# A running log-sum-exp: the last column chunk kept in place, its total handed on through the next tile's first row

## The chip, the cores and the metric

The kernel runs on one core of a Trainium2 chip. The metric is the device time of one execution in microseconds (us). Engines are named as in the profile: PE is TensorE's matmul, PEld its weight load, DVE is VectorE, ACT is ScalarE, POOL is GpSimd, SP is SyncE, whose queue issues every transfer of the main loop; the transfers themselves run on 16 DMA engines.

## The reference

```python
B, S, D = (4, 4096, 4128)          # float32
out[:, 0, :] = x[:, 0, :]
for t in range(1, S):
    mx = np.maximum(out[:, t - 1, :], x[:, t, :])
    out[:, t, :] = mx + np.log(np.exp(out[:, t - 1, :] - mx) + np.exp(x[:, t, :] - mx))
```

Each output row is the logarithm of the sum of the exponentials of all input rows up to it, for every batch and column. Without the maximum, which is there for range alone, that is Ln of a running sum of Exp along S.

## The kernel before

A tile (a `Step`) holds 128·r consecutive rows of one batch, r rows in each of 128 partitions, so partition p holds rows p·r to p·r+r-1 and all 4128 columns; r is 2 or 3 (the lists `begin`, `usual` and `final` give r of each tile of the first, middle and last batch). There are 49 tiles: 30 with 3 rows and 19 with 2. They go round four slots in SBUF; the first slot has room for 2 rows, the others for 3.

A tile's columns are worked in three chunks of 1376 (`Chunk`, `NC` = 3). For each chunk:

- `exp` (L106): ScalarE takes Exp of the chunk in place. On the first tile of a batch a Relu pass over row 0 (L109) adds up, for the range test, how far values lie below a bound.
- `sums` (L118, L120): VectorE adds a partition's rows. The second-to-last row then holds the sum of the rows before it, and the work tile `z` of that chunk gets the whole partition's sum, for partitions 0 to 126. Partition 127 of `z` is left alone: it still holds the last running sum of the tile before.
- `head` (L128): TensorE multiplies `z` by a matrix, `below` in a batch's first tile and `carried` in the others, in three column pieces. The product in PSUM, p, is for each partition the running sum ahead of its first row: the sums of the partitions below it, and what the previous tile carried. Two PSUM tiles take turns.
- `add` (L137, L145; L140 in a batch's last tile): VectorE adds that base to the rows but the last, and then forms the last row's running sum in `z`, whose partition 127 carries into the next tile.
- `log` (L150, L151): ScalarE takes Ln of the first rows in place and Ln of `z` into the last row.

At the end a test of range decides whether a slow general path (`_general`) has to run; with this input it does not.

The order of work is written by hand. Four lists, for transfers (`move`), ScalarE (`act`), VectorE (`vec`) and TensorE (`pe`), are emitted as they stand; `needs` says what an item depends on, and each engine runs its list in order. `usual_turn` and `last_turns` say how many `exp` of the next tile are put behind each `log` of this one, and how many `sums` ahead of each `add`:

```python
    usual_turn = (1, 2, 2), (0, 0, 1)
```

So after `log` of chunk 0 there is one `exp` of the next tile, and after `log` of chunk 1 a second. `moves` has the four first loads, then store 0, store 1, load 4, store 2, load 5 and so on; ahead of the end two loads stand together. All go through SP's queue (L89 and L92 loads, L95 stores), which waits in order: a load waits until the store that frees its slot has landed. Loads of tiles 0 to 4 are issued row by row (L92), later ones whole (L89).

Of the kernel before, what the change touches and what calls it, by code (L numbers as in the profile page):

```python
# [21 lines left out]
def kernel(  # L22
# [5 lines left out]
    nc = tc.nc  # L28
    B, S, D = x.shape
    assert S % P == 0 and D % (NC * 32) == 0  # L30
    CH = D // NC
# [5 lines left out]
    x2 = ctx.enter_context(tc.tile_pool(name="x2", bufs=1))  # L37
    x3 = ctx.enter_context(tc.tile_pool(name="x3", bufs=1))
# [22 lines left out]
    short = consts.tile([1, B * NC], FP32, name="short")  # L61
    spare = consts.tile([1, CH + 8], FP32, name="spare")[:, :CH]
    tiny = consts.tile([1, 1], FP32, name="tiny")
    nc.gpsimd.memset(short, 0.0)
    nc.gpsimd.memset(tiny, SMALL)

    z = [zpool.tile([P, CH], FP32, name=f"z{c}") for c in range(NC)]
# [10 lines left out]
    class Step:  # L78
# [17 lines left out]

    class Chunk:
        def __init__(self, step, c):
            self.t, self.c, self.z = step, c, z[c]
            self.pt = sides[(step.n * NC + c) % 2]  # L100
            self.cols = slice(c * CH, (c + 1) * CH)

        def exp(self):
            t = self.t
            e = t.xt[:, :, self.cols]
            nc.scalar.activation(e, e, ACT.Exp)  # L106
            if t.first:
                k = t.b * NC + self.c
                nc.scalar.activation(  # L109
                    spare, t.xt[0:1, 0, self.cols], ACT.Relu, bias=tiny, scale=-1.0,  # L110
                    accum_out=short[:, k:k + 1],
                )

        def sums(self):
            r = self.t.r
            e = [self.t.xt[:, j, self.cols] for j in range(r)]
# [3 lines left out]
            nc.vector.tensor_tensor(  # L120
                out=self.z[0:n], in0=e[r - 2][0:n], in1=e[r - 1][0:n], op=ALU.add,
            )

        def head(self):
            pt = self.pt
            w = below if self.t.first else carried
            for a, b in cuts:
                nc.tensor.matmul(  # L128
                    pt[:, a:b], lhsT=w, rhs=self.z[:, a:b], start=True, stop=True,
                )  # L130

        def add(self):
            t, r = self.t, self.t.r
            k = t.b * NC + self.c
            e = t.xt[:, 0:r - 1, self.cols]
            base = self.pt.unsqueeze(1).to_broadcast([P, r - 1, CH])
            nc.vector.tensor_tensor(out=e, in0=base, in1=e, op=ALU.add)  # L137
            ends = (t.xt[:, r - 2, self.cols], t.xt[:, r - 1, self.cols])
            if t.last:
                nc.vector.tensor_tensor_reduce(  # L140
                    out=self.z, in0=ends[0], in1=ends[1], scale=1.0, scalar=0.0,
                    op0=ALU.add, op1=ALU.add, accum_out=probe[:, k:k + 1],
                )
            else:
                nc.vector.tensor_tensor(out=self.z, in0=ends[0], in1=ends[1], op=ALU.add)  # L145

        def log(self):
            t, r = self.t, self.t.r
            e = t.xt[:, 0:r - 1, self.cols]
            nc.scalar.activation(e, e, ACT.Ln)  # L150
            nc.scalar.activation(t.xt[:, r - 1, self.cols], self.z, ACT.Ln)  # L151
# [16 lines left out]
    n = len(steps)  # L168
# [3 lines left out]
    for t in range(n):  # L172
# [17 lines left out]
    given = {"exp": [0] * (n + 1), "sums": [0] * (n + 1)}  # L190

    def upto(l, what, t, k):
        while given[what][t] < k:
            l.append((what, t, given[what][t]))
            given[what][t] += 1

    upto(act, "exp", 0, 2)
    for t in range(n):
        exps, sums = last_turns.get(t, usual_turn)
        upto(act, "exp", t, NC)  # L200
        upto(vec, "sums", t, 2)
        for c in range(NC):
            act.append(("log", t, c))
            upto(act, "exp", t + 1, (exps + (0,))[c])
            upto(vec, "sums", t + 1, sums[c])
            vec.append(("add", t, c))
            if c == 0:
                upto(vec, "sums", t, NC)
            pe.append(("head", t, c))

    def needs(what, t, c=None):
        if what == "load":
            return [("store", t - SLOTS)]
        if what == "store":
            return [("log", t, c) for c in range(NC)]
        return {
            "exp": [("load", t)],
            "sums": [("exp", t, c), ("log", t - 1, c)],
            "head": [("sums", t, c), ("add", t - 1, c)],
            "add": [("head", t, c)],  # L220
            "log": [("add", t, c)],
        }[what]

    done, at = set(), {e: 0 for e in lists}
    while any(at[e] < len(l) for e, l in lists.items()):
# [17 lines left out]
        out=fits[:, :B * NC], in0=probe, scalar1=LARGE, scalar2=None, op0=ALU.is_le,  # L243
    )
    nc.vector.tensor_scalar(
        out=fits[0:1, B * NC:], in0=short, scalar1=0.0, scalar2=None, op0=ALU.is_le,
    )
    low = consts.tile([P, 1], FP32, name="low")
    nc.vector.tensor_reduce(out=low, in_=fits, op=ALU.min, axis=AX.X)  # L249
# [7 lines left out]

    wrong = nc.values_load(flag[0:1, 0:1], min_val=0, max_val=1)  # L258
    with tc.If(wrong > 0):
        _general(tc, x, out)  # L260


def _general(tc, x, out):
# [8 lines left out]
    with tc.tile_pool(name="gpool", bufs=1) as pool:  # L272
        state = pool.tile([n, B, W], FP32, name="state")
        nc.scalar.dma_start(out=state, in_=rows(x, 0))
        nc.scalar.dma_start(out=rows(out, 0), in_=state)
        with tc.For_i(1, S, 1) as t:
            new = pool.tile([n, B, W], FP32, name="new")
            top = pool.tile([n, B, W], FP32, name="top")
            nc.scalar.dma_start(out=new, in_=rows(x, t))
            nc.vector.tensor_tensor(out=top, in0=state, in1=new, op=ALU.max)  # L280
            nc.vector.tensor_tensor(out=state, in0=state, in1=top, op=ALU.subtract)
            nc.vector.tensor_tensor(out=new, in0=new, in1=top, op=ALU.subtract)
            nc.scalar.activation(state, state, ACT.Exp)
            nc.scalar.activation(new, new, ACT.Exp)
            nc.vector.tensor_tensor(out=state, in0=state, in1=new, op=ALU.add)
            nc.scalar.activation(state, state, ACT.Ln)
            nc.vector.tensor_tensor(out=state, in0=state, in1=top, op=ALU.add)
            nc.scalar.dma_start(out=rows(out, t), in_=state)
# [1 line left out]
_INS = ['x']  # L290
_OUTS = [((4, 4096, 4128), 'float32')]
# [25 lines left out]
```

## Time and profile before

| what | value |
| --- | --- |
| time, median of 3 runs | 1260.23 us (1259.92 to 1260.83) |
| the profiled execution's own time | 1260.1 us |
| its span, first to last instruction | 1258.3 us |
| busy: DVE, ACT, PE | 956.0, 955.3, 604.8 us |
| moved by DMA | 541.28 MB, mean 430 GB/s |
| granted TensorE clock, mean | 0.686 |

Busy times are shares of one execution's span and can overlap freely, as the engines run side by side; an engine that is busy for 76% of the span may still be the one that is waited for in some stretch. A row of operations gives line, engine, shapes and count, then busy time and the mean ns of one, then how long the engine sat idle just before such operations and what ended that. DMA share is the mean busy share of the 16 DMA engines.

### The profile page before, as it was taken

What the parts mean: (1) busy time and instruction counts of PE and PEld (TensorE: products, weight loads), DVE (VectorE), ACT (ScalarE), POOL (GpSimd) and SP (SyncE); (2) the same over time, 40 slices, a digit from 0 to 9 for tenths busy, and PEclk for the clock granted to TensorE, in tenths of its full rate; (3) what the DMA queues carried; (4) which work ended last, traced back from release to release, by engine and by line L of the source; (5) the groups of instructions that cost most, each with busy time, mean ns of one, the idle gap of its engine ahead of it and who ended that gap; (6) DMA issues with size and microseconds to landing.
All of it is one profiled execution on the core that took longest, in us unless ns stands there. A gap on an engine that the chain in (4) does not pass through costs nothing.

```text
span 1258.3 us, 3243 instructions
## 1 busy us (share of the span) xinstructions
PE 604.8 (48%) x884; PEld 234.7 (19%) x884; DVE 956.0 (76%) x548; ACT 955.3 (76%) x466; POOL 4.6 (0%) x14
## 2 busy tenths in 40 slices
PE   3663454453555356245363435634635554464461
PEld 1221121121212122112121112211211221121120
DVE  3997696795967699579597679967957976795793
ACT  6987686786976698578697668867968966896792
POOL 1000000000000000000000000000000000000000
PEclk9877766666766666767667776756666675666686
DMA  9999999999999999999999999999999999999998
GB/s 399 424 439 425 434 437 427 434 434 428 440 423 443 429 434 436 433 432 435 433 427 433 438 433 432 437 427 437 436 430 435 431 434 431 435 435 433 433 439 351
DMA packets 14995, 541.28 MB, mean 430 GB/s; under 512 B 1664, under 2 KB 1664, under 8 KB 1664
## 3 DMA queue, kind: packets, MB, share of 16 engines
q1 hardware_dynamic: 14976, 541.07, 99.6%
q8 instruction: 7, 0.11, 0.0%
q14 instruction: 12, 0.10, 0.0%
HBM read 270.53 MB, written 270.53 MB: 430 GB/s over the span
## 4 chain that ended last, share of the span: by engine, by line
DMA 69%; DVE 14%; ACT 14%; issue 1%; PE 1%; SPq 0%; ACTq 0%; DVEq 0%
DMA x<-in_x_dram 49%; DMA out_dram<-x 19%; ACT x L106 6%; DVE x L137 6%; ACT x L150 4%; DVE z L120 3%; DVE z L145 3%; ACT x L151 3%; DVE x L118 2%; PE p L128 1%; DVE z L140 0%; SPq L95 0%; SPq L92 0%; ACTq L150 0%; ACTq L258 0%
## 5 line engine op out<-in xcount | busy, mean ns | idle before, releaser
L128 PE MATMUL p<-z,carried 128*128 128x512 f32 (+1 forms) x810 | 552.8, 843 | 542.7 <-DVE z L120 542.7
L106 ACT ACTIVATE x<-x 128x4128 f32<-128x4128 f32 (+1 forms) x147 | 468.0, 3187 | 219.5 <-DMA x<-in_x_dram 219.5
L128 PEld LDWEIGHTS p<-z,carried 128*128 128x128 f32 x810 | 214.4, 281 | 882.1 <-DVE z L120 646.8
L137 DVE TENSOR_TENSOR x<-p,x 128x2752 f32<-128x2752 f32 (+1 forms) x147 | 361.9, 2462 | 5.6 <-PE p L128 5.6
L150 ACT ACTIVATE x<-x 128x2752 f32<-128x2752 f32 (+1 forms) x147 | 300.6, 2045 | 62.8 <-DVE z L145 59.2
L118 DVE TENSOR_TENSOR x<-x 128x1376 f32<-128x1376 f32 x90 | 142.9, 1587 | 217.6 <-ACT x L106 217.6
L120 DVE TENSOR_TENSOR z<-x 127x1376 f32<-127x1376 f32 x147 | 233.9, 1591 | 52.4 <-ACT x L106 48.3
L145 DVE TENSOR_TENSOR z<-x 128x1376 f32<-128x1376 f32 x135 | 215.0, 1592 | 4.6
L151 ACT ACTIVATE x<-z 128x1376 f32<-128x1376 f32 x147 | 196.0, 1334 | 0.0
L128 PE MATMUL p<-z,below 128*128 128x512 f32 (+1 forms) x72 | 51.8, 886 | 85.1 <-DVE z L120 85.1
L128 PEld LDWEIGHTS p<-z,below 128*128 128x128 f32 x72 | 20.2, 298 | 115.2 <-DVE z L120 75.1
L140 DVE CUSTOM_DVE_ANT_0 z<-x 128x1376 f32<-128x1376 f32 x12 | 19.1, 1592 | 0.4
L109 ACT ACTIVATE spare<-x,tiny 1x1376 f32<-1x1376 f32 x12 | 17.3, 1442 | 0.4
L69 POOL MEMSET z<- 128x1376 f32 x3 | 3.7, 1240 | 0.0
L109 ACT ACTIVATION_READ_ACCUMULATOR spare<-x,tiny 1x1 f32 x12 | 2.2, 186 | 0.0
L251 PE MATMUL good<-ones,low 128*1 128x1 f32 x2 | 0.2, 164 | 4.2 <-DVE low L249 4.2
L34 ACT ACT_TABLE_LOAD x1 | 1.3, 1283 | 0.8 <-PEq L301 0.8
L140 DVE DVE_READ_ACCUMULATOR2_ANT probe<- 128x1 f32 x12 | 1.0, 83 | 0.0
L251 PEld LDWEIGHTS good<-ones,low 128*1 128x1 f32 x2 | 0.1, 80 | 4.7 <-DVE low L249 4.7
L253 DVE TENSOR_SCALAR flag<-good 1x1 int32<-1x1 f32 x1 | 0.1, 145 | 0.3 <-PE good L251 0.3
L51 POOL TENSOR_SCALAR_AFFINE_SELECT carried<-below 128x128 f32<-128x128 f32 x1 | 0.3, 290 | 0.0
L45 POOL TENSOR_SCALAR_AFFINE_SELECT below<-below 128x128 f32<-128x128 f32 x1 | 0.3, 285 | 0.0
(13 smaller groups left out, 1.6 us busy)
## 6 DMA issues: line engine op xcount, KB each, us to landing
out_dram<-x SPq DMA_DIRECT2D x30, 6192.0 KB, 24.9
x<-in_x_dram SPq DMA_DIRECT2D x29, 6192.0 KB, 38.2
out_dram<-x SPq DMA_DIRECT2D x19, 4128.0 KB, 21.4
x<-in_x_dram SPq DMA_DIRECT2D x15, 4128.0 KB, 33.4
x<-in_x_dram SPq DMA_DIRECT2D x11, 2064.0 KB, 20.7
```

The costliest lines, as they stand in the source:

```text
L34: nc.scalar.preload_act_table_set("natural_log_exp_and_others")
L69: nc.gpsimd.memset(t, 0.0)
L106: nc.scalar.activation(e, e, ACT.Exp)
L109: nc.scalar.activation(spare, t.xt[0:1, 0, self.cols], ACT.Relu, bias=tiny, scale=-1.0, accum_out=short[:, k:k + 1],)
L118: nc.vector.tensor_tensor(out=e[1], in0=e[0], in1=e[1], op=ALU.add)
L120: nc.vector.tensor_tensor(out=self.z[0:n], in0=e[r - 2][0:n], in1=e[r - 1][0:n], op=ALU.add,)
L128: nc.tensor.matmul(pt[:, a:b], lhsT=w, rhs=self.z[:, a:b], start=True, stop=True,)
L137: nc.vector.tensor_tensor(out=e, in0=base, in1=e, op=ALU.add)
L140: nc.vector.tensor_tensor_reduce(out=self.z, in0=ends[0], in1=ends[1], scale=1.0, scalar=0.0, op0=ALU.add, op1=ALU.add, accum_out=probe[:, ...
L145: nc.vector.tensor_tensor(out=self.z, in0=ends[0], in1=ends[1], op=ALU.add)
L150: nc.scalar.activation(e, e, ACT.Ln)
L151: nc.scalar.activation(t.xt[:, r - 1, self.cols], self.z, ACT.Ln)
```

## The change

The third chunk (`PASSED` = 2) loses its work tile. Its `sums` leave the partition's sum in the tile's own last row, for all 128 partitions. `head` multiplies that row by a new matrix, `summed`: `below` with its column 0 set to ones. So row 0 of the product, where the base of partition 0 would stand, holds the whole tile's total. `add` is a single three-operand instruction in place over all r rows: product times `inner` (1, but 0 in partition 0, so that the total is not added to the tile's own rows), plus the rows. `log` is one Ln over all rows. A new step, `fold`, carries the total on: VectorE adds row 0 of the product to row 0 of the next tile's first partition, after its Exp and ahead of its sums; so the carried sum is part of the next tile's total too. In the last tile of a batch `total` reduces row 0 of the product for the range test. For the test at a batch's first tile `least` (a minimum on VectorE, for each chunk) takes the place of the Relu pass.

The room that this frees makes the fourth slot as large as the others. The tile lists are new: 46 tiles, 36 with 3 rows and 10 with 2. Tiles 0 to 6 are loaded row by row. The turns are new as well, and their counts of `exp` now apply ahead of each `log`, with a fourth count behind the last one. The general path borrows the work tiles' room instead of having its own; it still does not run.

```diff
+BY_ROW = 7
+PASSED = NC - 1
...
+    summed = consts.tile([P, P], FP32, name="summed")
+    nc.gpsimd.affine_select(
+        out=summed, in_=below, pattern=[[1, P]], compare_op=ALU.not_equal,
+        fill=1.0, base=0, channel_multiplier=0,
+    )
+    inner = consts.tile([P, 1], FP32, name="inner")
+    nc.gpsimd.memset(inner, 1.0)
+    nc.gpsimd.memset(inner[0:1, :], 0.0)
...
-    slots = [x2.tile([P, 2, D], FP32, name="x0")]
-    slots += [x3.tile([P, 3, D], FP32, name=f"x{k}") for k in range(1, SLOTS)]
+    slots = [xpool.tile([P, 3, D], FP32, name=f"x{k}") for k in range(SLOTS)]
...
-            if self.n > SLOTS:
+            if self.n >= BY_ROW:
                 nc.sync.dma_start(out=self.xt, in_=self.dram(x))
...
+            self.z = self.row[-1] if self.passed else z[c]
...
+        def least(self):
+            nc.vector.tensor_reduce(
+                out=short[:, self.k:self.k + 1], in_=self.row[0][0:1], op=ALU.min, axis=AX.X,
+            )
+        def fold(self):
+            to = self.row[0][0:1]
+            pt = sides[(self.t.n * NC + self.c - NC) % 2]
+            nc.vector.tensor_tensor(out=to, in0=pt[0:1], in1=to, op=ALU.add)
+        def total(self):
+            nc.vector.tensor_reduce(
+                out=probe[0:1, self.k:self.k + 1], in_=self.pt[0:1], op=ALU.add, axis=AX.X,
+            )
...
-            n = P - 1
+            n = P if self.passed else P - 1
...
-            w = below if self.t.first else carried
+            w = summed if self.passed else below if self.t.first else carried
...
+            if self.passed:
+                base = self.pt.unsqueeze(1).to_broadcast([P, r, CH])
+                nc.vector.scalar_tensor_tensor(
+                    out=self.e, in0=base, scalar=inner[:, 0:1], in1=self.e,
+                    op0=ALU.mult, op1=ALU.add,
+                )
+                return
...
+            if self.passed:
+                nc.scalar.activation(self.e, self.e, ACT.Ln)
+                return
...
-    begin = [2, 2, 2, 3, 2, 3, 2, 3, 2, 3, 3, 3, 2]
-    usual = [3, 2, 3, 2, 3, 3, 3, 2, 3, 3, 3, 2]
-    final = [3, 3, 3, 2, 3, 3, 3, 2, 3, 3, 2, 2]
+    begin = [2, 2, 3, 3, 3, 3, 3, 3, 3, 3, 2, 2]
+    usual = [2, 3, 3, 3, 3, 3, 3, 3, 3, 3, 3]
+    final = [2, 3, 3, 3, 3, 3, 3, 3, 3, 2, 2, 2]
...
-    usual_turn = (1, 2, 2), (0, 0, 1)
-    last_turns = {
-        n - 5: ((0, 0, 0), (0, 0, 0)),
-        n - 4: ((0, 2, 3), (0, 0, 0)),
-        n - 3: ((2, 3, 3), (0, 0, 1)),
-        n - 2: ((2, 3, 3), (0, 0, 1)),
+    usual_turn = (0, 2, 3, 3), (0, 0, 1, 1)
+    turns = {
+        0: ((2, 3, 3, 3), (0, 0, 1, 1)),
+        1: ((1, 2, 2, 2), (0, 0, 0, 0)),
+        2: ((3, 3, 3, 3), (0, 0, 0, 0)),
+        3: ((2, 2, 3, 3), (0, 0, 0, 0)),
+        n - 3: ((0, 0, 3, 3), (0, 0, 0, 0)),
+        n - 2: ((1, 2, 3, 3), (0, 0, 1, 1)),
```

In VectorE's list `fold` (or `least`, or `total`) of the third chunk stands behind the tile's `sums` of chunk 1 and ahead of `add` of chunk 0. A product may not start until the `fold` that reads its PSUM tile is through.

More of the change, by code (lines that the diff above doesn't have):

```diff
@@ L98, in __init__ @@
         def __init__(self, step, c):
-            self.t, self.c, self.z = step, c, z[c]
+            self.t, self.c = step, c
+            self.passed = c == PASSED
             self.pt = sides[(step.n * NC + c) % 2]
             self.cols = slice(c * CH, (c + 1) * CH)
+            self.k = step.b * NC + c
+            self.e = step.xt[:, :, self.cols]
+            self.row = [step.xt[:, j, self.cols] for j in range(step.r)]
+            self.z = self.row[-1] if self.passed else z[c]
         def exp(self):
[L104 to L112, printed above, removed]
+            nc.scalar.activation(self.e, self.e, ACT.Exp)
+        def least(self):
[10 more added lines that the diff above has]
+            )
         def sums(self):
-            r = self.t.r
-            e = [self.t.xt[:, j, self.cols] for j in range(r)]
+            r, e = self.t.r, self.row
             if r == 3:
                 nc.vector.tensor_tensor(out=e[1], in0=e[0], in1=e[1], op=ALU.add)
-            n = P - 1
+            n = P if self.passed else P - 1
             nc.vector.tensor_tensor(
@@ L137, in add @@
             nc.vector.tensor_tensor(out=e, in0=base, in1=e, op=ALU.add)
-            ends = (t.xt[:, r - 2, self.cols], t.xt[:, r - 1, self.cols])
+            ends = self.row[r - 2], self.row[r - 1]
             if t.last:
@@ L215, in needs @@
             return [("log", t, c) for c in range(NC)]
+        if what == "head":
+            u, d = divmod(t * NC + c - 2, NC)
+            need = [("sums", t, c), ("add", u, d)]
+            if d == PASSED and u >= 0:
+                need.append(("total", u, d) if steps[u].last else ("fold", u + 1, d))
+            return need if c == PASSED else need + [("add", t - 1, c)]
+        if what == "sums":
+            need = [("exp", t, c)]
+            if c != PASSED:
+                return need + [("log", t - 1, c)]
+            return need if steps[t].first else need + [("fold", t, c)]
+        if what == "add":
+            return [("head", t, c)] + ([("least", t, c)] if steps[t].first else [])
         return {
             "exp": [("load", t)],
-            "sums": [("exp", t, c), ("log", t - 1, c)],
-            "head": [("sums", t, c), ("add", t - 1, c)],
-            "add": [("head", t, c)],
+            "fold": [("exp", t, c), ("head", t - 1, c)],
+            "total": [("head", t, c)],
+            "least": [("exp", t, c)],
             "log": [("add", t, c)],
@@ L259, with _general @@
     with tc.If(wrong > 0):
-        _general(tc, x, out)
-def _general(tc, x, out):
+        _general(tc, x, out, z)
+def _general(tc, x, out, room):
     nc = tc.nc
@@ L270, in rows, with part @@
         return t[:, bass.ds(at, 1), :].rearrange("b o (p d) -> p (o b) d", d=W)
[L272 to L288, printed above, removed]
+    def part(t, at):
+        return t[:n, at * B * W:(at + 1) * B * W].rearrange("p (b d) -> p b d", d=W)
+    state, new, top = part(room[0], 0), part(room[0], 1), part(room[1], 0)
+    nc.scalar.dma_start(out=state, in_=rows(x, 0))
+    nc.scalar.dma_start(out=rows(out, 0), in_=state)
+    with tc.For_i(1, S, 1) as t:
+        nc.scalar.dma_start(out=new, in_=rows(x, t))
+        nc.vector.tensor_tensor(out=top, in0=state, in1=new, op=ALU.max)
+        nc.vector.tensor_tensor(out=state, in0=state, in1=top, op=ALU.subtract)
+        nc.vector.tensor_tensor(out=new, in0=new, in1=top, op=ALU.subtract)
+        nc.scalar.activation(state, state, ACT.Exp)
+        nc.scalar.activation(new, new, ACT.Exp)
+        nc.vector.tensor_tensor(out=state, in0=state, in1=new, op=ALU.add)
+        nc.scalar.activation(state, state, ACT.Ln)
+        nc.vector.tensor_tensor(out=state, in0=state, in1=top, op=ALU.add)
+        nc.scalar.dma_start(out=rows(out, t), in_=state)
 _INS = ['x']
```

63 lines of the change are left out of this document (37 added, 26 removed).

## The prediction

> **What bounds the kernel now.** I read the page first for engines and transfers, then the chain that ended last, then stretches of the start, the middle and the end, then the rows of single operations.
>
> Engines and transfers, from the page (shares of the span; tenths of a slice; queue: packets, MB, share of 16 engines):
>
> ```profile
> span 1258.3 us, 3243 instructions
> PE 604.8 (48%) x884; PEld 234.7 (19%) x884; DVE 956.0 (76%) x548; ACT 955.3 (76%) x466; POOL 4.6 (0%) x14
> DMA  9999999999999999999999999999999999999998
> q1 hardware_dynamic: 14976, 541.07, 99.6%
> q8 instruction: 7, 0.11, 0.0%
> q14 instruction: 12, 0.10, 0.0%
> ```
>
> No compute engine passes 76%, and the 16 DMA engines are busy in every slice. The first line of the chain of waits says the same:
>
> ```profile
> DMA 69%; DVE 14%; ACT 14%; issue 1%; PE 1%; SPq 0%; ACTq 0%; DVEq 0%
> ```
>
> The stretches tell whether those busy engines also move bytes at an even rate (last columns: DMA share, GB/s):
>
> ```profile
> 0.00:5.00 5.00, 0.00 (x0) 0.00 (x0) 0.00 (x0) 1.28 (x1) 4.37 (x14) 1.00 0.65 225
> 104.40:1240.00 1135.60, 550.41 (x794) 212.93 (x794) 880.04 (x502) 873.60 (x418) 0.00 (x0) 0.67 1.00 433
> 1250.00:1255.00 5.00, 0.00 (x0) 0.00 (x0) 0.00 (x0) 0.00 (x0) 0.00 (x0) 0.50 0.57 244
> 1255.00:1258.30 3.30, 0.00 (x0) 0.00 (x0) 0.00 (x0) 0.00 (x0) 0.00 (x0) 0.50 0.02 10
> ```
>
> At 433 GB/s the 541.07 MB take 1249.6 us. The other 8.7 us are the first 2.4 us (225 GB/s over 5 us is 2.6 us of full flow), a thinning end, and little else. The end thins because the 16 engines do not finish together: the sixteen increments of the last store's semaphore, one from each engine, run from 1251.57 to 1257.44 us in the trace. One engine is 5.9 us behind the first; it was 0.8 us behind at 88 us and 2.9 us at 104. So the span is the start, one engine's share of the transfers, and its lag.
>
> The transfers, from the page, and the last issue on SP's queue, from the timeline:
>
> ```profile
> out_dram<-x SPq DMA_DIRECT2D x30, 6192.0 KB, 24.9
> x<-in_x_dram SPq DMA_DIRECT2D x29, 6192.0 KB, 38.2
> out_dram<-x SPq DMA_DIRECT2D x19, 4128.0 KB, 21.4
> x<-in_x_dram SPq DMA_DIRECT2D x15, 4128.0 KB, 33.4
> x<-in_x_dram SPq DMA_DIRECT2D x11, 2064.0 KB, 20.7
> ...
> 1238.77 0.33 SPq L95 DMA_DIRECT2D out_dram<-x  x1
> ```
>
> That is 104 transfers. At 433 GB/s a 3-row transfer takes 14.64 us, a 2-row one 9.76, one row 4.88; landings in the middle follow each other at just these distances, so a queued transfer shows no fixed cost. A packet shows a small one: 16,512, 33,024 and 49,536 bytes take 0.615, 1.222 and 1.829 us in the trace, that is 0.607 us a row and 0.008 us a packet.
>
> The rows that the compute is priced by:
>
> ```profile
> L106 ACT ACTIVATE x<-x 128x4128 f32<-128x4128 f32 x90 | 326.6, 3632 | 186.4 <-DMA x<-in_x_dram 186.4
> L137 DVE TENSOR_TENSOR x<-p,x 128x2752 f32<-128x2752 f32 x90 | 271.6, 3018 | 3.3 <-PE p L128 3.3
> L120 DVE TENSOR_TENSOR z<-x 127x1376 f32<-127x1376 f32 x147 | 233.9, 1591 | 52.4 <-ACT x L106 48.3 <-ACT x L151 0.2
> L150 ACT ACTIVATE x<-x 128x2752 f32<-128x2752 f32 x90 | 224.3, 2492 | 49.9 <-DVE z L145 49.2
> L151 ACT ACTIVATE x<-z 128x1376 f32<-128x1376 f32 x147 | 196.0, 1334 | 0.0
> ```
>
> ScalarE sits idle 186 us for loads before its Exp: compute waits for data, not data for compute.
>
> **The bytes and the packets.** Bytes are unchanged. Transfers: 46 stores; loads by row for tiles 0 to 6 (2+2+3+3+3+3+3 = 19); 39 whole loads; together 104 again. Each is 128 packets, so both kernels send 13,312 data packets, 832 per engine, and the 3 stores and 5 whole loads saved (49 to 46, 44 to 39) are the 8 more single-row loads. Cost 0.0 us.
>
> **VectorE.** Per 3-row tile now: 3 x (1.587 + 1.591 + 3.018 + 1.592) = 23.4 us; per 2-row tile 3 x (1.591 + 1.584 + 1.592) = 14.3. After it, two chunks stay (15.6 and 9.5). Chunk 2 has its sums (3.18 or 1.59), a fold on one partition and the three-operand add in place. The fold shows nowhere: bounds 0.153 us (a 1x12 VectorE row) and 1.592; I take 1.59, its length being 1376. The new add over 4128 elements from PSUM: 3.02 at least (2752), 4.45 by the step from 1.584 to 3.018, 8.9 if its two operations cost two passes; I take 4.45 (3.02 for 2 rows), as one element a cycle is what every two-input row shows, the one that adds and accumulates (1.592 for 1376) included. So 24.8 and 15.7 us per tile. With 36 and 10 tiles, and 12 minima and 4 totals of 1.59 less the folds they replace, VectorE's sum goes from 973 to about 1065 us, 85% of the span. Cover: a pair of 3-row transfers lasts 29.3 us, so 4.5 us per tile are left; without it each microsecond above 29.3 would cost 36 us in all.
>
> **ScalarE.** It loses twelve Relu passes (17.3 + 2.2 us), and a chunk's two Ln become one (3.83 to about 3.63 us, by the Exp row). The sum goes from 30 x 22.4 + 19 x 15.5 + 19.5 = 986 to 36 x 22.2 + 10 x 15.3 = 952 us, all beside transfers: 0.0.
>
> **The waits that the new order makes.** On ScalarE all three Exp of tile t+1 now stand ahead of the last Ln of tile t, so store t waits for load t+1 and then 3 x 3.63 + 3.83 + 3.63 = 18.35 us. Queued behind that Ln are only the next tile's Ln; behind the store on SP is load t+3. A landing is seen 1.0 us after its last byte (first Exp at 13.19; two rows from 2.4 us would end at 12.16), and an issue flows 1.6 us later (0.80 to 2.4). Together 21 us. Meanwhile the queue holds store t-1 and load t+2: 29.3 us in the run of 3-row tiles, slack 8 us; 24.4 us at the seven places where one of the two has 2 rows, slack 3.3. VectorE's part (Exp 3.63, sums 3.18, new add 4.45) ends 3.4 us before ScalarE reaches that Ln. The fold waits for the third Exp, about 14.7 us after it can see the load, and holds a PSUM buffer of the next product: sums, adds and the fold behind it end at about 28 us, before the next landing plus Exp. It hides.
>
> At the end the cover shrinks. After the last load, now two 3-row and one 2-row store run before the last one (39.0 us, of which 31.2 from landing 1207.6 to the issue at 1238.77, 2.6 latencies: slack 5.2). Changed: one 3-row and two 2-row stores, 34.2 us. Chain: 1.0, three Exp and two pairs of Ln (12.8), fold 1.59, add 3.18, sum 1.59, product 4.11 (604.8/147), add 3.02, Ln 2.49, 1.6: 31.4. Slack 2.8 us. Cost 0.0, but this is the tightest place.
>
> At the start four loads are 10 rows rather than 9, so the first store may come 4.9 us later before the queue runs dry; the second had almost none left. Gain 0.0 to 0.5; I take 0.0.
>
> **Instructions.** Three fewer tiles are 54 fewer matmuls with as many weight loads; with the Relu passes and the merged Ln about 98 ScalarE instructions go: some 206 of 3243. The 19 refills on q8 and q14 move 16 or 8 KB through one engine, 0.3 to 0.6 us each. One fewer on the lagging engine: -0.4 us; bounds -1.2 and 0.
>
> **Sum.** Span 1258.3 + 0.0 - 0.4 = 1257.9; the profiled execution took 1260.1 us, 1.8 outside the span: 1259.7. The median shown is 1260.23, 0.1 above the profiled one: 1259.8.
>
> **Rivals.** About 0.2% (2.5 us) is what a measurement can tell from no change here.
>
> 1. Faster: the lag of the last engine shrinks. Its jump of 2 us at 88 to 104 us falls where whole-tile loads begin, and the change loads two more tiles by row. For it: the rate outside is even, so this is all there is to win. Against: refills stay, and the lag also grew later (3.9 us by 280, 4.9 by 1160). With a lag of 2 us: 1259.8 - 3.5 = 1256.3; with none 1254. The Trainium skill ("Runtime: NRT & Kernel Launch", Instruction fetch mechanics) says that a sequencer fetches its next 16 KiB block over its own DMA queue, mostly hidden; q8's 0.11 MB in 7 packets agrees in size, and by "hidden" the lag would not depend on it: the 0.4 us would be 0, and the sum 1260.2. Chance 0.15.
>
> 2. Slower: store t comes too late. Place: the end and the seven 24.4 us covers. It decides once the chain from landing to issue is over 2.8 us (end) or 3.3 us (each of the seven) longer than summed. At 4 us longer: 1.2 + 7 x 0.7 = 6.1, so 1266; at 3.5: 0.7 + 1.4, so 1262. For it: waits between engines are summed at nothing, and the early phase has its own hand-set turns. Against: the same sort of sum, for the old end, leaves 5 us, and the trace shows no thinning before 1250. Chance 0.12.
>
> 3. VectorE becomes the bound: the new add takes two passes. 24.8 + 4.45 = 29.2 us per tile against 29.3, with waits on top. VectorE's 1065 + 36 x 4.45 + 10 x 3 = 1255 us, plus the 15.8 before its first sum and some 20 after its last: 1290. Nothing in its rows speaks for it. Chance 0.03.
>
> 4. The new lists reach the same transfers in another order than the sum assumes; that would show as rival 2. No chance of its own.
>
> **Numbers.** Forecast 0.70: 1259.8. Its own bounds are the lag's (-1.5, +1.5). From the rivals: faster 0.15, same 0.70, slower 0.15 (0.12 + 0.03). The range takes in rival 1 down to a lag of about 2.7 us (1257.0) and rival 2 up to 3.7 us longer chains (0.9 + 7 x 0.4 = 3.7 us: 1263.5, rounded up).
>
> **What would show it.** Right: 104 transfers, DMA at 433 GB/s from 104 us on, VectorE near 85%, the new add at 4.4 us, last landings spread by 4 to 7 us, last store issued before the one ahead of it has flowed out. Wrong: a slice of the DMA row below 9 inside the span, SP's store issues over 21 us after the load's landing, a new add near 9 us, or a spread below 3 us with the span under 1255.5.

## The result: 5 us slower

| | median | runs | range |
| --- | --- | --- | --- |
| before | 1260.12 us | 6 | 1259.77 to 1260.83 |
| after | 1265.14 us | 6 | 1262.61 to 1266.84 |

The ratio is 1.0038, with a 95% interval of 1.0023 to 1.0052. The forecast was 1259.8 us, with a range of 1257.0 to 1264.0. The execution that was profiled took 1262.61 us, the fastest of the six; so its trace holds 2.3 of the 5.0 us (span 1260.6 against 1258.3), and what the longer executions add was not traced.

Engines and transfers of the changed kernel, from its page (columns as before):

```profile
span 1260.6 us, 3131 instructions
PE 601.3 (48%) x830; PEld 233.9 (19%) x830; DVE 1047.2 (83%) x547; ACT 926.1 (73%) x369; POOL 3.8 (0%) x15
DMA  9999999999999999999999999999999999999998
q1 hardware_dynamic: 14976, 541.07, 99.7%
q14 instruction: 11, 0.09, 0.0%
```

The first line of its chain of waits:

```profile
DMA 61%; ACT 22%; DVE 9%; issue 6%; SPq 1%; ACTq 0%; DVEq 0%
```

The same stretches as before (last columns: DMA share, GB/s):

```profile
0.00:5.00 5.00, 0.00 (x0) 0.00 (x0) 0.00 (x0) 1.28 (x1) 3.76 (x15) 1.00 0.66 221
104.40:1240.00 1135.60, 556.20 (x756) 215.50 (x756) 959.23 (x495) 844.04 (x334) 0.00 (x0) 0.66 1.00 432
1250.00:1255.00 5.00, 0.00 (x0) 0.00 (x0) 0.00 (x0) 0.00 (x0) 0.00 (x0) 0.50 0.96 416
1255.00:1260.60 5.60, 0.00 (x0) 0.00 (x0) 0.00 (x0) 0.00 (x0) 0.00 (x0) 0.50 0.30 130
```

The transfers, and the last issue on SP's queue, from the timeline:

```profile
out_dram<-x SPq DMA_DIRECT2D x36, 6192.0 KB, 26.0
x<-in_x_dram SPq DMA_DIRECT2D x31, 6192.0 KB, 40.1
out_dram<-x SPq DMA_DIRECT2D x10, 4128.0 KB, 22.0
x<-in_x_dram SPq DMA_DIRECT2D x19, 2064.0 KB, 28.2
x<-in_x_dram SPq DMA_DIRECT2D x8, 4128.0 KB, 34.7
...
1242.82 0.33 SPq L99 DMA_DIRECT2D out_dram<-x  x1
```

The rows that the compute was priced by, with the shapes kept apart:

```profile
L113 ACT ACTIVATE x<-x 128x4128 f32<-128x4128 f32 x108 | 388.8, 3632 | 155.2 <-DMA x<-in_x_dram 155.2
L150 DVE SCALAR_TENSOR_TENSOR x<-p,inner,x 128x4128 f32<-128x4128 f32 x36 | 162.3, 4510 | 0.6 <-PE p L142 0.5
L123 DVE TENSOR_TENSOR x<-p,x 1x1376 f32<-1x1376 f32 x42 | 66.1, 1573 | 2.8 <-ACT x L113 2.4
L150 DVE SCALAR_TENSOR_TENSOR x<-p,inner,x 128x2752 f32<-128x2752 f32 x10 | 30.8, 3077 | 0.0
```

Little on these pages looks wrong. There are 104 transfers and 14,976 packets as before, all 16 DMA engines are busy in every slice, ScalarE is still the one that waits for loads; only the chain that ended last now spends 22% of the span in ScalarE, 14% before. Yet the rate from 104 to 1240 us is 432 GB/s instead of 433: one part in 433 of 1135.6 us is 2.6 us, about what the spans differ by (both rates are rounded). The loss is in the flow of the transfers, not at the start or the end.

The trace's packet records say in which form. Per engine (mean of 16) the time without a packet, between its first and its last, sums to 0.70 us, 0.63 before. But the packets of 16,512, 33,024 and 49,536 bytes, which take 0.615, 1.222 and 1.829 us when undisturbed, took 6.55 us longer than that in sum, 3.06 before. So the engines did not starve; some of their packets were **stretched**. That is the whole loss: from its first packet to its last an engine took 1255.0 us in the mean, 1251.5 before. (The span grew by 2.3 us only, as the last engine's end came closer to the others'.) And the stretching is not even: in certain loads 13 to 21 packets, late in the load and so about one of each engine, are 0.2 to 1.0 us longer, all begun within some 4 us. Before has no load with more than 0.08 us of this per engine after 210 us; after has 0.56 us in load 35, 0.41 in load 36, 0.82 in load 38 and 0.77 in load 45.

Such a load can be seen landing late on ScalarE. These are Exp operations of the changed kernel (L113) that waited for a load, and one Ln (L169), from its timeline (start, duration, engine, line, tiles, and in brackets the idle time before and what ended it):

```profile
984.92 7.18 ACT L113 ACTIVATE x<-x 128x4128 f32<-128x4128 f32 x2 [6.89 <-DMA x<-in_x_dram]
...
999.16 3.63 ACT L169 ACTIVATE x<-x 128x4128 f32<-128x4128 f32 x1
...
1039.53 7.18 ACT L113 ACTIVATE x<-x 128x4128 f32<-128x4128 f32 x2 [5.74 <-DMA x<-in_x_dram]
...
1068.66 7.18 ACT L113 ACTIVATE x<-x 128x4128 f32<-128x4128 f32 x2 [4.74 <-DMA x<-in_x_dram]
...
1097.92 7.18 ACT L113 ACTIVATE x<-x 128x4128 f32<-128x4128 f32 x2 [4.87 <-DMA x<-in_x_dram]
```

The last two distances are 29.13 and 29.26 us, a pair of 3-row transfers (2 x 14.64 = 29.28). Between the first two Exp lie a 2-row store, load 37, a 3-row store and load 38: 9.76 + 3 x 14.64 = 53.68. They are 54.61 apart: 0.93 us late.

What went before it is on SP's queue, from the timeline of its issues:

```profile
1002.82 0.34 SPq L99 DMA_DIRECT2D out_dram<-x  x1
1003.25 0.38 SPq L93 DMA_DIRECT2D x<-in_x_dram  x1
```

Store 35 is issued at 1002.82, just when the last Ln (999.16 + 3.63) is through, and load 38 right behind it. At that time load 37 was the only work left in the queue. Its semaphore's increments come from 1004.3 us (first engine) to 1009.2 (last). So the first engine had 1.5 us left. I call this the **lead** of a store: the time from its issue until the first engine ends the transfer queued ahead of it, taken from the first increment of that transfer's semaphore. In before, the leads are 4.4 us or more in the main run; only its last stores, which stand behind stores, have less (4.2, 3.9 and 3.1 us). In after, seven stores behind loads have 3.0 us or less. Six of them are followed by a stretched load, as a rule the one that was issued together with the store; the 0.06 us after load 26 is no more than before has:

| load ahead | 10 | 15 | 23 | 26 | 34 | 37 | 43 |
| --- | --- | --- | --- | --- | --- | --- | --- |
| lead of the store behind it, us | 3.0 | 2.3 | 2.7 | 2.8 | 2.4 | 1.5 | 1.9 |
| stretch of the load behind that, us per engine | 0.13 | 0.23 | 0.11 | 0.06 | 0.56 | 0.82 | 0.77 |

In the last column that load is not the one issued with the store: load 44, with 2 rows, was, and it is not stretched (0.01). Load 45 is, which was issued 21 us later with 5.3 us to spare.

Theory: a store that is issued less than some 3 us before the queue begins to run out costs up to some 1 us, paid a pair of transfers later, though no engine runs dry. Rivals: A, the new compute's traffic or its order of transfers slows the packets; B, the stretching is chance.

The theory of leads was formed only after experiments 1 to 4. When those were set up, the first theory was the order of transfers, and late stores stood as "Rival B" of experiment 2; the expectations of 1 to 4 go by those names, "new theory" from 5 on is the one of leads.

### The profile page after: what moved, and what is told of

It is laid out like the page before. It is cut to its first block, busy times and chain, and to the rows that moved or that the text cites. A ratio compares the mean times of both kernels' runs of the same rounds, so it can differ in the third digit from the quotient of the medians.

```text
span 1260.6 us, 3131 instructions
## 1 busy us (share of the span) xinstructions
PE 601.3 (48%) x830; PEld 233.9 (19%) x830; DVE 1047.2 (83%) x547; ACT 926.1 (73%) x369; POOL 3.8 (0%) x15
## 3 DMA queue, kind: packets, MB, share of 16 engines
q1 hardware_dynamic: 14976, 541.07, 99.7%
## 4 chain that ended last, share of the span: by engine, by line
DMA 61%; ACT 22%; DVE 9%; issue 6%; SPq 1%; ACTq 0%; DVEq 0%
DMA x<-in_x_dram 57%; ACT x L113 11%; ACT x L169 5%; ACT x L173 4%; DMA out_dram<-x 4%; DVE x L150 2%; ACT x L174 2%; DVE x L157 2%; DVE z L135 1%; DVE x L133 1%; DVE z L160 1%; DVE x L135 0%; DVE x L123 0%; SPq L99 0%; DVE short L116 0%
## 5 line engine op out<-in xcount | busy, mean ns | idle before, releaser
L113 ACT ACTIVATE x<-x 128x4128 f32<-128x4128 f32 (+1 forms) x138 | 462.3, 3382 | 183.7 <-DMA x<-in_x_dram 183.6
L142 PE MATMUL p<-z,carried 128*128 128x512 f32 (+1 forms) x504 | 375.2, 910 | 456.4 <-DVE z L135 297.0
L173 ACT ACTIVATE x<-x 128x2752 f32<-128x2752 f32 (+1 forms) x92 | 206.0, 2239 | 129.7 <-DVE z L165 117.1
L133 DVE TENSOR_TENSOR x<-x 128x1376 f32<-128x1376 f32 x108 | 171.2, 1585 | 146.8 <-ACT x L113 146.8
L142 PE MATMUL p<-x,summed 128*128 128x512 f32 (+1 forms) x276 | 194.3, 867 | 130.9 <-issue 125.1
L157 DVE TENSOR_TENSOR x<-p,x 128x2752 f32<-128x2752 f32 (+1 forms) x92 | 248.2, 2698 | 0.9 <-PE p L142 0.8
L150 DVE SCALAR_TENSOR_TENSOR x<-p,inner,x 128x4128 f32<-128x4128 f32 (+1 forms) x46 | 193.1, 4198 | 0.6 <-PE p L142 0.5
L135 DVE TENSOR_TENSOR z<-x 127x1376 f32<-127x1376 f32 x92 | 146.3, 1590 | 39.5 <-ACT x L113 33.7
L169 ACT ACTIVATE x<-x 128x4128 f32<-128x4128 f32 (+1 forms) x46 | 155.5, 3379 | 2.4 <-DVE x L150 2.4
L165 DVE TENSOR_TENSOR z<-x 128x1376 f32<-128x1376 f32 x84 | 133.8, 1592 | 2.9
L142 PEld LDWEIGHTS p<-x,summed 128*128 128x128 f32 x276 | 75.3, 290 | 248.5 <-issue 245.9
L135 DVE TENSOR_TENSOR x<-x 128x1376 f32<-128x1376 f32 x46 | 73.2, 1590 | 1.2
```

What stands on the lines that cost most here:

```text
L113: nc.scalar.activation(self.e, self.e, ACT.Exp)
L135: nc.vector.tensor_tensor(out=self.z[0:n], in0=e[r - 2][0:n], in1=e[r - 1][0:n], op=ALU.add,)
L142: nc.tensor.matmul(self.pt[:, a:b], lhsT=w, rhs=self.z[:, a:b], start=True, stop=True,)
L150: nc.vector.scalar_tensor_tensor(out=self.e, in0=base, scalar=inner[:, 0:1], in1=self.e, op0=ALU.mult, op1=ALU.add,)
L169: nc.scalar.activation(self.e, self.e, ACT.Ln)
```

## The experiments

Each kernel ran beside before on the same chip, whose medians were 1260.29 to 1260.32 us.

**1. The changed kernel again**, unaltered.

> The changed kernel once more, unaltered. First theory (transfers are stretched where loads give way to stores, by the regular order of 3-row transfers): about 1265 us again, between 1262 and 1267, the DMA engines never idle in the middle, and packets of 49,536 bytes over 1.829 us in bursts of 10 to 20 at the ends of loads, at much the same tiles as before (35, 36, 38, 45). Rival A (compute traffic slows transfers): the same time, but bursts anywhere. Rival B (chance, not the kernel): near 1260 in some runs, and bursts in the kernel before as well.

Measured: 1265.56 us (1263.27 to 1266.22), ratio 1.0040 (1.0027 to 1.0053). The loads behind the short leads are stretched again: 35 (0.51), 38 (0.89), 45 (0.69), 24 (0.31), 16 (0.18), 11 (0.18). Load 36, which has no short lead ahead of it, is not this time. B falls.

**2 and 3. Only the transfers**, in the order of the changed kernel (46 tiles) and of the one before (49).

```diff
-    lists = {"move": moves, "act": [], "vec": [], "pe": []}
...
+    lists = {"move": moves}
...
-            return [("log", t, c) for c in range(NC)]
+            return [("load", t)]
```

> Leaves out all compute: each tile of the 46-tile order is loaded and stored back unchanged, in the same order of transfers on the same queue. First theory: the stretching is in the order of transfers alone, so this takes 3 to 5 us more than the same copy in the order of 49 tiles. Rival A (VectorE's and ScalarE's traffic in SBUF): both copies within 1 us of each other, near 1255 to 1258 us. Rival B (late stores leave too little queued): both copies equal as well, since a store here never waits for compute.

> Leaves out all compute: the 49-tile order of the kernel before as a bare copy. First theory: 3 to 5 us faster than the copy in the order of 46 tiles. Rivals A and B: within 1 us of it. If compute costs the kernel before nothing, about 1258 to 1260 us.

Measured: 1259.31 us (1258.88 to 1261.44) and 1258.18 us (1257.64 to 1259.26). The new order costs 1.1 us by itself, not the 3 to 5 of the first theory; with stores issued some 30 us ahead or more, up to the last load, no load is stretched by more than 0.15 us after 300 us. The order falls as the main cause.

**4. The new compute with the old tiles and slots.**

```diff
-BY_ROW = 7
+BY_ROW = 5
...
-    slots = [xpool.tile([P, 3, D], FP32, name=f"x{k}") for k in range(SLOTS)]
+    slots = [x2.tile([P, 2, D], FP32, name="x0")]
+    slots += [x3.tile([P, 3, D], FP32, name=f"x{k}") for k in range(1, SLOTS)]
...
-    begin = [2, 2, 3, 3, 3, 3, 3, 3, 3, 3, 2, 2]
+    begin = [2, 2, 2, 3, 2, 3, 2, 3, 2, 3, 3, 3, 2]
...
-        n - 3: ((0, 0, 3, 3), (0, 0, 0, 0)),
+        n - 4: ((0, 0, 3, 3), (0, 0, 0, 0)),
+        n - 3: ((0, 2, 3, 3), (0, 0, 1, 1)),
```

> The new compute (third chunk in place, fold, minima on VectorE) with the old slots, the old 49 tiles and the old five row-by-row tiles; the last turns are set for this order. First theory: back near 1260 us, plus at most 3 us because the last store of this order is issued late by my sum of rows. Rival A (compute traffic): as slow as the changed kernel, 1264 to 1267 us, with bursts spread over the span.

Measured: 1270.08 us (1263.34 to 1273.83), ratio 1.0076 (1.0056 to 1.0095). The first theory expected some 1260 to 1263 us, so the old order does not bring the time back. It has more places with a 2-row tile in the queue, and leads of 1.0 to 2.4 us ahead of the stretched loads 37 (0.38), 41 (0.31) and 45 (0.50). Leads of 2.9 and 3.0 us, at loads 24 and 32, are followed by nothing. But so are leads of 2.4, 2.1 and 2.4 us, at loads 19, 35 and 39: the 2-row loads issued with those stores have 0.01 us at most, and the store after each has a short lead of its own. So it fits the theory in part and does not part it from A, and its profiled execution, the fastest (1263.34), cannot show what made four of the others 6 to 10 us longer.

**5. Six of the changed kernel's stores earlier**: one Exp less ahead of the last Ln.

```diff
+        8: ((0, 2, 2, 3), (0, 0, 0, 1)),
+        13: ((0, 2, 2, 3), (0, 0, 0, 1)),
+        21: ((0, 2, 2, 3), (0, 0, 0, 1)),
+        24: ((0, 2, 2, 3), (0, 0, 0, 1)),
+        32: ((0, 2, 2, 3), (0, 0, 0, 1)),
+        35: ((0, 2, 2, 3), (0, 0, 0, 1)),
```

> The changed kernel with one thing undone at six places: in tiles 8, 13, 21, 24, 32 and 35 the third Exp of the next tile goes behind the last Ln of this tile, so their stores go out about 3.6 us sooner. The new theory (a store that is issued under some 3 us before the first DMA engine ends the load ahead of it is followed, one transfer pair later, by stretched packets on all engines): the bursts at the ends of loads 11, 16, 24, 35 and 38 go, the one at load 45 stays, and the time falls by 2 to 4 us, to 1261 to 1263. Rival A (the in-place compute and its traffic): unchanged at 1265.

Measured: 1262.25 us (1261.19 to 1262.96), ratio 1.0014 (1.0005 to 1.0023): some 3 us of the 5 come back. Leads at loads 34 and 37 are now 4.2 us and loads 35 and 38 are no longer stretched (0.01 us). Four short leads are left, or new: 2.9 us behind load 27, then nothing (0.01); 2.8 us behind load 11, then 0.21 us in load 12; 2.1 us behind load 38, then 0.52 us in load 39; and -0.5 us behind load 43, the first engines idle, then 0.89 us in load 45.

**6. The kernel before with late stores**: none of the new compute, only one Exp more ahead of the second and the third chunk's Ln.

```diff
-    usual_turn = (1, 2, 2), (0, 0, 1)
+    usual_turn = (2, 3, 3), (0, 0, 1)
```

(The old turn stays for tiles 0 to 3, 12 and 24.)

> The kernel before, its compute and tiles untouched, with all three Exp of the next tile ahead of the last Ln (turn (2, 3, 3) instead of (1, 2, 2), but for tiles 0 to 3, 12 and 24), so that some sixteen stores are issued about 3.5 us later, 1 to 3 us before the load ahead of them ends. New theory: bursts behind those places and 1263 to 1268 us, though nothing of the in-place change is in it. Rival A: 1260, as before.

Measured: 1265.38 us (1264.95 to 1268.79), ratio 1.0041 (1.0027 to 1.0055). The profiled execution took 1268.79 us, the longest of the five. Leads of 0.7 to 2.1 us are followed by loads stretched by 0.5 to 0.9 us, at six places; stretch in all 11.6 us, time without a packet 1.1. (One of 1.9 us, at load 31, is followed by nothing in the 2-row load issued with its store, as in experiment 4.) The long window from 104 us on, of this kernel:

```profile
104.40:1240.00 1135.60, 544.18 (x788) 210.09 (x789) 873.09 (x492) 863.56 (x414) 0.00 (x0) 0.67 1.00 430
```

A falls: the loss comes without the in-place chunk, its fold or its tiles, by lateness alone.

**7 and 8. The copy of experiment 2 with stores held back** by dummy ScalarE passes, once to about the leads of the changed kernel and once four passes (5.5 us) fewer.

```diff
+        def wait(self):
+            u = steps[min(self.n + 1, len(steps) - 1)]
+            nc.scalar.activation(slow[:, :8], u.xt[:, u.r - 1, :8], ACT.Identity)
+            for _ in range({(3, 3): 15, (3, 2): 12, (2, 3): 13, (2, 2): 10}[self.r, u.r] - 2):
+                nc.scalar.activation(slow, slow, ACT.Identity)
...
-            return [("load", t)]
+            return [("wait", t)]
```

> Leaves out all compute but a chain of dummy ScalarE passes on a private tile: the bare 46-tile copy, with each store held back behind the next tile's load and that chain for about as long as in the changed kernel (13 passes for two 3-row tiles, 8 to 11 otherwise), so that stores go out 1 to 3 us before the load ahead of them ends at the seven places. New theory: bursts and 2 to 6 us more than the bare copy's 1259.3. Rival A: 1259 to 1260, since VectorE and TensorE do nothing.

> The same copy with four passes fewer in each chain, so stores go out about 5.5 us sooner and no margin is under 5 us. New theory: no bursts after the first 60 us, 1259 to 1260 us. Rival A: the same. If this is slow as well, it is the chain and not its end that matters.

Measured: late 1266.67 us (1265.93 to 1267.0), early 1258.98 (1258.51 to 1259.54). The same instructions and transfers but for the four passes; 7.7 us apart. The late one lies above its expected range, and its leads came out shorter than meant: 0.6 to 2.8 us at the seven places, 1.5 to 3.0 in the changed kernel; in the early one all are 7.3 us or more. The long window of the late one, then of the early one:

```profile
104.40:1240.00 1135.60, 0.00 (x0) 0.00 (x0) 0.00 (x0) 689.41 (x586) 0.00 (x0) 1.00 1.00 430
```

```profile
104.40:1240.00 1135.60, 0.00 (x0) 0.00 (x0) 0.00 (x0) 464.81 (x419) 0.00 (x0) 1.00 1.00 433
```

Stretch 10.3 against 3.3 us per engine, time without a packet 0.5 against 0.1. The early one's 3.3 us are mostly in loads 0 (0.73), 3 (0.61) and 7 (0.50): before 300 us a load or two is stretched in most of these kernels, without a short lead, and why is open. DMA share 1.00 in both: full queues and full engines are not yet a full rate.

**9. The changed kernel with every lead over 4 us** up to the last load: the fold behind the add of chunk 0, one Exp less ahead of the last Ln.

```diff
-    usual_turn = (0, 2, 3, 3), (0, 0, 1, 1)
+    usual_turn = (0, 2, 2, 3), (0, 0, 0, 1)
...
+        42: ((0, 2, 3, 3), (0, 0, 1, 1)),
...
-            if c == PASSED - 1:
+            if c == PASSED - 1 and not 5 <= t <= 42:
                 passing(t)
...
             vec.append(("add", t, c))
+            if c == 0 and 5 <= t <= 42:
+                passing(t)
```

> The changed kernel with the same tiles, slots and operations, but in tiles 5 to 42 the fold stands behind the add of chunk 0 (in the changed kernel ahead of it), and one Exp less of the next tile stands ahead of the last Ln, so that every store from tile 4 to 42 should be issued 5 us or more before the load ahead of it begins to run out. Late-issue theory: no stretched packets after 300 us and the time of this order of transfers without any late store, which the copy with early stores gave as 1258.98 us, plus the start and end of the full compute: 1259.3 to 1260.5, level with the kernel before and 5 us under the changed kernel. If something else in the new compute costs the time (its traffic, its VectorE load, the four equal slots), it stays at 1262 to 1265 us although the stores are early.

Measured: 1260.86 us (1260.46 to 1261.79), ratio 1.0005 (0.9996 to 1.0014): level with before, 4.3 us under the changed kernel, and 0.4 us above the expected range. SP's issue of store 35:

```profile
999.07 0.34 SPq L99 DMA_DIRECT2D out_dram<-x  x1
```

It comes at 999.07 instead of 1002.82, lead 4.8 us, and load 38 is not stretched (0.00). The loads at all seven places are stretched by 0.04 us at most. Loads 31 (0.40) and 17 (0.26) are stretched though no short lead stands before them, against the expectation; so something else can stretch a load as well, and I did not find what. This version does not beat before, nor can it by much: the copy of its transfers takes 1259 us.

**10, 11 and 12. Where and how much.** In the copy with early stores, first stores 26, 34, 37 and 43 alone were delayed; then all stores by an amount between early and late; then stores 24, 32, 35 and 41 alone.

```diff
+LATE = 24, 32, 35, 41
...
+            late = self.n in LATE
+            for _ in range({(3, 3): 15, (3, 2): 12, (2, 3): 13, (2, 2): 10}[self.r, u.r] - (2 if late else 6)):
```

> No Exp, sum, product or Ln: the tiles are only copied, in the changed kernel's order of transfers, with dummy ScalarE passes that time each store. Stores are early (as in the copy of 1258.98 us) except the four that wait behind loads 27, 35, 38 and 44 (tiles 26, 34, 37 and 43), which are as late as in the copy of 1266.67 us. If each late store costs by itself, once, packets are stretched only in loads 27, 35, 38 and 45, by 0.5 to 1.0 us per engine each, and the time is 1258.98 plus those four shares of the late copy (0.81 + 1.02 + 0.87 + 1.00 = 3.7 us): 1261.5 to 1263. If the stretching needs a queue that runs short all along, or comes with the place in memory, the time is under 1260, or the other loads are stretched too.

> The same copy, with every store one dummy pass of about 1.45 us earlier than in the copy of 1266.67 us, so that the six latest of them are issued some 2 to 3.7 us before the load ahead begins to run out, instead of 0.6 to 2.2. If the cost begins below 2.8 us, as the traces so far suggest, only the places under that are stretched (those of tiles 43 and 34, perhaps 26 and 15) and the time lies between, 1260 to 1264 us. If what decides is the queue running dry, at zero, the time is that of the early copy, 1259.0. If any store later than the early copy's costs the same, it stays at 1266.5.

> The copy of tiles (no Exp, sum, product or Ln) with early stores, except stores 24, 32, 35 and 41: these are the ones queued behind loads 26, 34, 37 and 43, where one of the two transfers in the queue has 2 rows, and they are issued 0.6 to 2 us before the load ahead begins to run out. (The run before it delayed stores 26, 34, 37 and 43 by as much; these still came 6.6 us or more ahead, and nothing changed.) If the short lead costs, at its own place and once, packets are stretched in loads 27, 35, 38 and 45 alone, by 0.5 to 1.0 us per engine each, and the time is 1258.98 plus the shares those loads had in the copy with all stores late (0.81 + 1.02 + 0.87 + 1.00 us): 1261.5 to 1263. If the stretching needs a queue that runs short all along, it stays at 1258.9.

Measured, 10: 1258.93 us (1257.98 to 1259.22). I had named the wrong stores: behind load 27 stands store 25, not 26, and the four that I delayed kept leads of 6 us or more. As a control it says that being 5.5 us later costs nothing while the lead stays long. 11: 1258.86 us (1258.45 to 1262.84); leads of 3.2 to 3.6 us at all the tight places after 300 us, and none stretched; one load (18, 0.42) is, without a short lead. The leads came out longer than the 2 to 3.7 us expected, so no place fell under the edge, and the time, that of the early copy, does not decide between the first two expectations; with the leads of 2.4 us that cost elsewhere, the edge lies somewhere near 3 us. 12: 1263.53 us (1263.11 to 1264.72), 4.6 us above the copy without late stores, a little over the expected range. Leads 1.4, 2.0, 1.3 and 2.0 us; stretched after 300 us are load 27 (0.79), 35 (0.65), 38 (1.07) and 45 (0.73), with their stores (0.44, 0.08, 0.43, 0.11), and no other: 4.3 us.

Store 24's pair in this kernel, on SP's queue:

```profile
690.00 0.34 SPq L102 DMA_DIRECT2D out_dram<-x  x1
```

The landings around it, on ScalarE, where each dummy chain waits for a load; with store 24 late:

```profile
696.06 0.21 ACT L106 ACTIVATE z<-x 128x8 f32<-128x8 f32 x1 [6.08 <-DMA x<-in_x_dram]
...
726.06 0.21 ACT L106 ACTIVATE z<-x 128x8 f32<-128x8 f32 x1 [17.26 <-DMA x<-in_x_dram]
...
755.23 0.21 ACT L106 ACTIVATE z<-x 128x8 f32<-128x8 f32 x1 [16.43 <-DMA x<-in_x_dram]
```

and in the copy with early stores:

```profile
695.69 0.21 ACT L105 ACTIVATE z<-x 128x8 f32<-128x8 f32 x1 [11.62 <-DMA x<-in_x_dram]
...
724.93 0.21 ACT L105 ACTIVATE z<-x 128x8 f32<-128x8 f32 x1 [16.50 <-DMA x<-in_x_dram]
...
754.17 0.21 ACT L105 ACTIVATE z<-x 128x8 f32<-128x8 f32 x1 [16.50 <-DMA x<-in_x_dram]
```

Early: 29.24 and 29.24 us. Late: 30.00 across the pair issued late, then 29.17. One late store, one late landing, at its own place and once. With that the cause of the loss is shown, by adding it (6, 7, 12) and by taking it away (5, 8, 9). It was lateness alone in 12, where an engine had 0.15 us without a packet in all, so the queue had not run dry. What inside the DMA engines stretches packets a pair of transfers after a late issue stays open.

## Why the prediction was wrong

**What held.** Transfers, packets and bytes: unchanged, as summed. VectorE: 1047 us, 83% (forecast sum 1065, 85%; its terms add up to some 1069); the new add is one pass, 4.51 us (4.45 taken), 3.08 with 2 rows (3.02), and the fold 1.57 (1.59), so rival 3 is out. ScalarE: 926 us busy, hidden. The start: nothing gained or lost. The instructions: those that the page lists by engine are 205 fewer (206 forecast), the whole count only 112, as other kinds grew by 93. One refill fewer on q14, as said; its 0.4 us cannot be told (in the packet records a refill takes 0.31 us on q14 and 0.9 to 1.1 on q8, where 0.3 to 0.6 was taken). Rival 1's lag did shrink, as its premise had it: the last store's increments run from 1254.98 to 1259.75 us, 4.8 us against 5.9. But it shrank because the first engine ended 3.4 us later; the gain that rival 1 saw in it did not follow.

**What failed** is the step "The waits that the new order makes", in the words "24.4 us at the seven places where one of the two has 2 rows, slack 3.3", and with it the 0.0 that the sum has for those waits: they cost 3.0 us of stretch in the profiled execution and most of the 5.0 in the median, by experiment 9. (24.4 less 21 is 3.4, which changes nothing.) The seven places were right, to the number: they are the seven of the table of leads. The chain was right too: from the Exp at 984.92 to the end of the last Ln at 1002.79 are 17.9 us, 18.35 in the sum. Two things about the slack were wrong.

First, against what it was measured. The sum ran from one landing to the next, that is to the last engine's end. The trace of before showed the engines spread by 2.9 to 5.9 us, and the prediction used that for the lag of the end alone. Store 35 had 1009.2 - 1002.82 = 6.4 us until the last engine was through with load 37, 4.8 after the 1.6 us that an issue takes to flow: more than the forecast's 3.3. Against the first engine, at 1004.3, it had 1.5 us, less than that 1.6 (the engine still went on without a pause; the packet records have the first packet of all 1.0 us after its issue). So the slack was shorter by the spread of the engines, 3.5 to 5 us, and it shrank as the spread grew: at all seven places the last engine had 6.2 to 6.5 us left, but the first one 3.0 at load 10, where the spread is 3.5, and 1.5 at 37, where it is 4.9. The Trainium skill ("DMA: Bandwidth & Descriptors", Queues, rings and completion order) says that each engine has a ring of its own in a queue; the spread of 4.9 us in load 37's increments agrees, and by that rule it is the ring that empties first that counts, not the last.

Second, what a short slack costs. The prediction took it as free until it is used up, and then as idle time. The Trainium skill ("DMA: Bandwidth & Descriptors", Anatomy of one DMA — SWDGE (gpsimd) path) says, of transfers that GpSimd issues, that the engines "just consume their queues". The traces here agree in that the engines went on without a pause (0.70 us without a packet in all, 0.63 before), but not at an even pace, of which that section says nothing. Measured: 0.06 to 0.13 us per engine at leads of 2.7 to 3.0 us, 0.2 to 1.1, with the store's share, at 1.5 to 2.4 in the changed kernel. Rival 2 had the place and the sign, but its point of decision ("over 2.8 us (end) or 3.3 us (each of the seven) longer than summed") was wrong: the chains were no longer than summed, and it decided all the same. That its 1266 us, for chains 4 us longer, lies near the measured time is luck, since it priced idle time. Seven loads, 2.7 us together, with store 35 (0.27) make 2.95 of the 3.5 us of added stretch in the profiled execution; load 36 (0.41) has no short lead ahead of it.

The **end**, called the tightest place, cost nothing: the last store was issued at 1242.82, 7.2 us before the last engine ended the store ahead, 2.4 before the first. With that lead, the last store was stretched by no more than 0.04 us; a pair of transfers later there is nothing left to stretch.

Of what "would show it": SP's store issues did not come over 21 us after the landing, no DMA slice is below 9 but the last, the spread is 4.8 us. All signs of "right" but one were there. The exception is 432 instead of 433 GB/s, and the text did not say that a change of one in that number is the whole effect.

**What is left.** Version 9 is 0.5 us above before, and the copy in the new order 1.1 us above the copy in the old; neither was taken apart further. Why the changed kernel's executions differ by 4 us among themselves, where those of before differ by 1, was not traced.

## What to carry to other kernels

Where one queue keeps all DMA engines busy, measure the lead of each issue against the engine that finishes first, not against the landing, which is the last engine's; and keep some 4 us (after 300 us, leads of 3.2 to 3.6 us were followed by loads with a stretch of 0.1 us at most). A hand-written order that moves work ahead of a store is paid at the place where the queue holds the least, here where one of two transfers is small. A DMA share of 1.00 does not prove the full rate: compare GB/s over the long window, or the distances of landings, with a copy that does nothing else.

## What the runs showed of the hardware

- A late issue is paid later: a store and load of 3 rows that are issued with a short lead have stretched packets at their own ends, 14 and 30 us after the issue (store 24 of experiment 12: issued at 690.0, stretched packets at 703 to 706 and 719 to 722 us), while the engines had no pause. Where the load has 2 rows, the stretch is in the load behind it (behind load 43 of the changed kernel: store issued at 1174.3, load 44 0.01 us, load 45 0.77).
- The price goes by the lead more than by the place in the run, but not by the lead alone: 0.06 to 0.23 us per engine at leads of 2.3 to 3.0 us and 0.56 to 0.82 at 1.5 to 2.4 in the changed kernel, where the short ones came late; in experiment 6, after leads of 1.4 and 2.1 us, 0.8 as early as 512 us; in experiment 4, at 2.1 to 2.4 us, from nothing to 0.5. In experiment 12, at 1.3 to 2.0 us, it was 0.7 to 1.5 us with the store's share.
- Transfers alone, with nothing else running, took 1258.2 us in the old order: the kernel before is within 2.1 us (0.17%) of that.
- A `scalar_tensor_tensor` of 4128 elements per partition from PSUM, in place, took 4.51 us: the next step of the two-operand adds from PSUM, 1.58 us for 1376 and 3.01 for 2752.
